# One kernel with two edits: DeltaNet chunks that keep their decays and keys and are merged in pairs, and SSD chunks that start with C·B and its mask

## The chip, the cores and the metric

The kernel runs on one core of a Trainium2 chip. The metric is device time in microseconds of one execution; lower is better. Engines are named as in the profile: PE (TensorE, matrix products), PEld (its weight loads), DVE (VectorE), ACT (ScalarE), POOL (GpSimd) and SP (SyncE, which issues most transfers).

## What is computed

One residual layer over 1024 tokens of width 1024, with 16 meta tokens ahead of them. A normalised input is projected to about 13,400 columns, which feed two token mixers; their gated outputs are merged, projected, added to the input and sent through a gated feed-forward part. Cut to what the change touches:

```python
# gated DeltaNet, per value head and chunk (8 q/k heads, 16 value heads, width 128)
a_low = strict_lower(k_beta @ k.T * decay)           # decay = exp(g_cum[l] - g_cum[s])
t_inv = inverse(a_low + eye)
qk    = (q @ k.T) * decay
v_new = t_inv @ (v*beta) - (t_inv @ (k_beta*exp(g_cum))) @ S
o     = (q*exp(g_cum)) @ S + qk @ v_new
S     = S * exp(g_cum[-1]) + (k*exp(g_cum[-1]-g_cum)).T @ v_new
# SSD, per group of 8 heads and chunk (4 groups, 32 heads of width 64, state 128)
scores = (C @ B.T) * decay
y      = scores @ (x*dt) + (C @ S) * exp(a_cum)
S      = S * exp(a_cum[-1]) + B.T @ (x*dt*decay_to_end)
```

All of it is float32. The large products are made of three products of a rounded high part and its remainder (`hi·hi`, `hi·lo`, `lo·hi`).

## The kernel before

The program is written out in full, with no loop on the chip. A tile framework places buffers from pools and decides, before the program runs, in which order each engine's instructions stand. Each engine then works through its own list in that order. A pool's `bufs` is the number of buffers that a name rotates through, and a new tile waits until the oldest buffer's last reader is done. PSUM has eight banks of 128x512 floats, tagged `psd` (two, for the dense products), `p` (two), and `a`, `b`, `o`, `z` (one each).

There are three stages. In the first, the 1040 columns (16 meta tokens and 8 chunks of 128) are projected, one weight tile of 128 output columns at a time (`dense_u`, `ztile`, `gate_tile`; lines 141 to 143 are the three products), and DeltaNet runs beside it. In the second, SSD runs beside the rest of the projection. In the third come the branch projections and the feed-forward part. "Dense product" below means one matrix product of lines 141 to 143 (in the changed kernel 143 to 145).

A weight tile (512 KB) is loaded by `load_w` into `wraw` (two buffers). ACT rounds it into `whi`, DVE subtracts to get `wlo` (two buffers each), and the tile after the present one is already asked for when a tile starts.

DeltaNet is done for eight sub-heads `i`, each one q/k head with two value heads:

- `dn_conv(i)` makes q, k and v tiles (projection, then a four-tap convolution). `squares` transposes q and k chunk by chunk into the bank `z`, where ACT squares and sums them.
- `dn_p1(i, c)` makes, for each chunk `c`, k·k and the decays of two heads (`decay`: a product with a selecting column and two kinds of ACT instruction), and from them the matrix `W` to be inverted.
- `dn_inv(i)` writes the 32x32 diagonal blocks of `W` to memory, reads them back as `X` with a block in each partition, inverts them on DVE in 30 steps (lines 537 and 539), writes them back (line 541), and reads them into `W` (line 546). Three DVE transposes make `T32` of them (line 550).
- `dn_merge(i, c)` joins the blocks to the whole inverse with products of 96, then 32 and 64 columns (lines 561, 565, 566, 572, 576), each of which waits for an ACT or DVE step after the one before.
- `dn_p2(i, c)` runs the recurrence over the chunks: k·S and q·S (lines 617 and 619), the product with `W` (629), the update of the state (637) and the output (639). It first makes the decays, q·k and the transposed k of the chunk again (lines 608, 609 and 418).
- `dn_z(i, h)` multiplies the finished output by a gate tile; its dense products fill a `psd` bank that is emptied only when the chunks' outputs are ready.

In the program's text a sub-head's conv tiles and `dn_p1` stand after the `dn_p2` of the one before.

Of the kernel before, what the change touches and what calls it, by code (L numbers as in the profile page):

```python
# [92 lines left out]
def body(tc, A):  # L93
# [35 lines left out]

    def load_w(src, kk=KD, room=None):  # L130
# [97 lines left out]
    convp = tkp.tile([128, len(CONV), 5], F32, name="convp")  # L228
    cvp = tc.tile_pool(name="cv", bufs=2)
# [269 lines left out]
    def dn_p1(i, c):  # L499
        d = sub[i]  # L500
        c0, L = cr(c)
        if c == 8:
            d["W"] = sb.tile([128, 8, 2, 128], F32, name="W")
            d["Wm"] = sb.tile([NM, 2, NM], F32, name="Wm")
        kT = d["qk"][:, 1, c0:c0 + L]
        ps = psm("p")
        E = sb.tile([128, 2, 128], F32, name="E")
        pe.matmul(ps[0:L, 256:256 + L], kT, kT, start=True, stop=True)
        decay(E, ps, rowD, selD, 32, (2 * i, 2 * i + 1), c)
        kkm = sb.tile([128, 128], F32, name="kkm")  # L510
        dve.tensor_tensor(kkm[0:L, 0:L], ps[0:L, 256:256 + L], stri[0:L, 0:L], op=ALU.mult)
        N = d["W"][:, c] if c < 8 else d["Wm"]
        for h in range(2):
            dve.scalar_tensor_tensor(N[0:L, h], E[0:L, h, 0:L], d["w"][0:L, c, h:h + 1], kkm[0:L, 0:L],
                                     op0=ALU.mult, op1=ALU.mult)
        nd = nd_dram[i]
        if c in (3, 7):
            for b in range(4):
                r = slice(32 * b, 32 * b + 32)
                for h in range(2):  # L520
                    sp.dma_start(V(nd[0:64], "(c h b) s l -> s c h b l", h=2, b=4)[:, c - 3:c + 1, h, b],
                                 d["W"][r, c - 3:c + 1, h, r])
# [3 lines left out]
    def dn_inv(i):  # L526

        d = sub[i]
        X = sb.tile([66, 32, 32], F32, name="X", bufs=1)
# [18 lines left out]
        for b in range(3):  # L548
            r = slice(32 * b, 32 * b + 32)
            dve.transpose(T32[r, :, r], V(d["W"][r, :, :, r], "s c h l -> s (c h) l"))  # L550

    def dn_merge(i, c):

        d = sub[i]
        W = d["W"]
        ps = psm("p")
        zz = sb.tile([128, 2, 3, 32], F32, name="zz")
        p10 = sb.tile([64, 2, 32], F32, name="p10")
        z4 = V(ps[:, 0:192], "p (h b s) -> p h b s", h=2, b=3)
# [8 lines left out]
        act.copy(W[0:32, c, :, 32:64], p4[0:32])  # L568
        act.copy(W[64:96, c, :, 96:128], p4[64:96])
        p5 = V(ps[:, 256:320], "p (h s) -> p h s", h=2)  # L570
        for h in range(2):
            pe.matmul(p5[64:128, h], W[32:64, c, h, 64:128], p10[32:64, h], start=True, stop=True)
# [665 lines left out]
```

## Time and profile before

| what | us |
|---|---|
| three timed runs | 3000.59, 3000.81, 3009.75 (median 3000.81) |
| profiled execution, its own time | 3007.62 |
| its span, first instruction to last | 3005.8 |
| PE busy in the span | 2916.2 |
| DVE busy | 1974.6 |
| ACT busy | 1324.3 |
| POOL busy | 289.3 |

The span is read along PE. A product's "busy" time in the profile reaches past the start of the next product, because products are pipelined. So what a product costs is read from the distance between starts in the view by time, and not from its mean duration. Instructions with float32 operands on both sides appear as two records per product, transposes and the dense products as one.

### The profile page before, as it was taken

To read this page: it belongs to the slowest core of one execution; us is meant where nothing else is said; L and a number is where in the kernel's file an instruction comes from. 1 tells how busy PE (TensorE), PEld (TensorE's weight loads), DVE (VectorE), ACT (ScalarE), POOL (GpSimd) and SP (SyncE) were. 2 spreads that over 40 slices of the span, in tenths; PEclk is the share of its full clock that TensorE was granted. 3 is DMA by queue.
4 is the path that set the end of the run, shared out by engine and by line. 5 is a ranking of instruction groups with operands and counts; after the bars stand their busy time and mean duration, and the time that the engine had idled before them with its cause. 6 is when DMAs were issued, how large, how long until landed. Compare 5 with 4: busy or idle time off the path is not lost.

```text
span 3005.8 us, 43124 instructions
## 1 busy us (share of the span) xinstructions
PE 2916.2 (97%) x16130; PEld 2452.7 (82%) x16130; DVE 1974.6 (66%) x3858; ACT 1324.3 (44%) x3319; POOL 289.3 (10%) x274
## 2 busy tenths in 40 slices
PE   7899999999999999999999999999999899999997
PEld 6788788888888879878888778888877688888886
DVE  8577787876867855776768653464568655555446
ACT  5546466456554544555546543212235233333213
POOL 2200000000000000001010100000000333330000
PEclk9999999999999999999999999999999899999998
DMA  3111111111211211111011115343353222226312
GB/s 105 43 57 37 50 50 35 58 50 29 64 33 47 68 43 54 35 57 56 33 60 36 70 61 172 102 139 110 112 182 105 97 80 84 81 81 226 96 53 74
DMA packets 119177, 227.32 MB, mean 76 GB/s; under 512 B 46984, under 2 KB 53800, under 8 KB 118968
## 3 DMA queue, kind: packets, MB, share of 16 engines
q1 hardware_dynamic: 117240, 222.47, 22.7%
q8 instruction: 127, 2.08, 0.3%
q10 hardware_dynamic: 1728, 2.10, 0.2%
q14 instruction: 82, 0.67, 0.1%
HBM read 175.14 MB, written 49.38 MB: 75 GB/s over the span
## 4 chain that ended last, share of the span: by engine, by line
PE 84%; DVE 9%; ACT 3%; DMA 1%; issue 1%; POOL 1%; SPq 0%; DVEq 0%; ACTq 0%; POOLq 0%
PE psd L142 15%; PE psd L143 15%; PE psd L141 15%; PE pq_p L1000 1%; PE pq_p L1001 1%; PE pq_p L1002 1%; PE ps_p L561 1%; PE ps_o L746 1%; PE pq_psd L1001 1%; PE ps_o L639 1%; PE pq_psd L1002 1%; PE pq_psd L1000 1%; PE ps_a L629 1%; PE ps_a L617 1%; PE ps_o L619 1%
## 5 line engine op out<-in xcount | busy, mean ns | idle before, releaser
L142 PE MATMUL psd<-u_lo,whi 128*128 128x512 f32 (+3 forms) x2136 | 770.8, 361 | 3.4 <-DVE u_lo L150 2.3
L141 PE MATMUL psd<-u_hi,whi 128*128 128x512 f32 (+3 forms) x2136 | 764.9, 358 | 1.6 <-ACT raw L374 1.6
L143 PE MATMUL psd<-u_hi,wlo 128*128 128x512 f32 (+3 forms) x2136 | 758.0, 355 | 4.0 <-DVE wlo L135 4.0
L134 ACT CAST whi<-wraw 128x1024 fp32r<-128x1024 f32 (+2 forms) x197 | 188.0, 955 | 649.1 <-PE psd L142 459.6
L142 PEld LDWEIGHTS psd<-u_lo,whi 128*128 128x128 f32 x2136 | 409.6, 192 | 41.3 <-issue 6.8
L143 PEld LDWEIGHTS psd<-u_hi,wlo 128*128 128x128 f32 x2136 | 406.1, 190 | 36.7 <-DVE wlo L135 4.5
L141 PEld LDWEIGHTS psd<-u_hi,whi 128*128 128x128 f32 x2136 | 405.2, 190 | 37.6 <-issue 4.0
L135 DVE TENSOR_TENSOR wlo<-wraw,whi 128x1024 fp32r<-128x1024 f32 (+2 forms) x197 | 217.8, 1106 | 153.5 <-ACT whi L134 147.4
L143 PE MATMUL psd<-blk,wlo 128*128 128x512 f32 x512 | 199.7, 390 | 1.2 <-DVE wlo L135 1.2
L141 PE MATMUL psd<-blk,whi 128*128 128x512 f32 x512 | 199.4, 390 | 0.0
L142 PE MATMUL psd<-blk,whi 128*128 128x512 f32 x512 | 199.4, 389 | 0.0
L374 ACT COPY raw<-psd 128x256 f32<-128x256 f32 x165 | 73.3, 444 | 93.1 <-PE psd L143 89.5
L143 PEld LDWEIGHTS psd<-blk,wlo 128*128 128x128 f32 x512 | 96.2, 188 | 21.8 <-DVE wlo L135 2.0
L906 DVE TENSOR_TENSOR part<-part,psd 128x512 f32<-128x512 f32 x96 | 65.7, 684 | 72.0 <-PE psd L143 72.0
L142 PEld LDWEIGHTS psd<-blk,whi 128*128 128x128 f32 x512 | 96.2, 188 | 20.1
L141 PEld LDWEIGHTS psd<-blk,whi 128*128 128x128 f32 x512 | 96.2, 188 | 19.8
L984 POOL TENSOR_TENSOR sw<-wraw 128x512 f32<-128x512 f32 x44 | 68.4, 1554 | 352.0 <-DMA wraw<-w_gu 240.5
L700 DVE TENSOR_TENSOR xdt<-ps_z,dtb 128x512 f32<-128x512 f32 (+1 forms) x36 | 24.8, 690 | 105.3 <-PE ps_z L697 105.3
L539 DVE TENSOR_TENSOR X<-X,itmp 66x30 f32<-66x30 f32 (+14 forms) x240 | 85.2, 355 | 5.2
L537 DVE TENSOR_TENSOR itmp<-X 66x30 f32<-66x30 f32 (+14 forms) x240 | 81.6, 340 | 5.8 <-DMA X<-nd 0.4
L99 POOL TENSOR_TENSOR qk<-raw,qk 128x400 f32<-128x400 f32 x16 | 30.4, 1900 | 537.6 <-ACT raw L380 423.3
L421 ACT ACTIVATE Es<-ps_p,cum 128x128 f32<-128x128 f32 x256 | 75.3, 372 | 11.1 <-PE ps_p L418 11.0
(686 smaller groups left out, 6277.7 us busy)
## 6 DMA issues: line engine op xcount, KB each, us to landing
wraw<-w_in SPq DMA_DIRECT2D x105, 512.0 KB, 3.3
wraw<-w_gu SPq DMA_DIRECT2D x48, 512.0 KB, 3.3
wraw<-w_br SPq DMA_DIRECT2D x36, 512.0 KB, 3.4
c<-hc SPq DMA_DIRECT2D x22, 512.0 KB, 2.7
hc<-c SPq DMA_DIRECT2D x22, 512.0 KB, 5.9
wraw<-w_dn SPq DMA_DIRECT2D x40, 256.0 KB, 2.6
g<-zt SPq DMA_DIRECT2D x32, 256.0 KB, 2.1
y_d<-zt SPq DMA_DIRECT2D x32, 256.0 KB, 2.0
```

Source lines behind the costliest of these rows:

```text
L134: act.copy(hi[:, 0:kk], raw[:, 0:kk])
L135: dve.tensor_tensor(lo[:, 0:kk], raw[:, 0:kk], hi[:, 0:kk], op=ALU.subtract)
L141: pe.matmul(ps[:, 0:n], hi[:, wk0 + k], ahi(k), start=(k == 0), stop=False)
L142: pe.matmul(ps[:, 0:n], hi[:, wk0 + k], alo(k), start=False, stop=False)
L143: pe.matmul(ps[:, 0:n], lo[:, wk0 + k], ahi(k), start=False, stop=(k == kk - 1))
L374: dense_u((name, lambda ps, p0, p1: act.copy(raw[:, 3 + p0:3 + p1], ps)))
L421: act.activation(E[0:L, i, 0:L], ps[0:L, 128 * i:128 * i + L], AF.Relu, bias=cum[0:L, c, h0 + h:h0 + h + 1], scale=-1.0)
L537: dve.tensor_tensor(t, X[:, 0:j, j:j + 1].broadcast_to([66, j, m]), X[:, j:j + 1, j + 1:32].broadcast_to([66, j, m]), op=ALU.mult)
L539: dve.tensor_tensor(X[:, 0:j, j + 1:32], X[:, 0:j, j + 1:32], t, op=ALU.add)
L906: dve.tensor_tensor(part[:, m, cs], part[:, m, cs], ps, op=ALU.add)
L984: pool.tensor_tensor(t, x, y, op=op)
L1000: pe.matmul(ps, w[0][:, k], y[0][:, k], start=start and k == 0, stop=False, skip_group_check=not start)
```

## The change

DeltaNet: `dn_p1` now also makes q·k, masks it and multiplies it into the decays `E`, which are kept for `dn_p2` (eight buffers). `squares` copies the transposed k out of the bank `z` four chunks at a time, and `dn_p2` and `dn_meta` read this copy. `dn_merge` joins two chunks (four matrices) at once. `W` is held in two halves with three buffers, `X` and `T32` share one buffer, `dn_p1` alternates between the banks `p` and `b`, and the blocks come back from memory in 16 transfers in place of 8. SSD: a chunk starts with C·B, its mask and the decays; the transposed input and the product for the state come later. The raw weight tile `wraw` has one buffer through the first two stages and two after them.

```diff
-        raw = wp.tile([128, KD, 128], F32, name="wraw", bufs=2)
+        raw = raws[0].tile([128, KD, 128], F32, name="wraw")
...
+    wrp = tc.tile_pool(name="wr1", bufs=1)
+    raws[0] = wrp.__enter__()
...
 squares:
+                pv = lambda c: ps[0:cr(c)[1], 128 * (c % 4):128 * (c % 4) + 128]
                 for c in cc:
                     c0, L = cr(c)
-                    pv = ps[0:L, 128 * (c % 4):128 * (c % 4) + 128]
-                    pe.transpose(pv, qk[:, j, c0:c0 + L], ident)
-                    act.activation(pv, pv, AF.Square, accum_out=ss[0:L, j, c:c + 1])
+                    pe.transpose(pv(c), qk[:, j, c0:c0 + L], ident)
+                if j == 1 and len(cc) > 1:
+                    d["kt", cc[0] // 4] = kt = sb.tile([128, 4, 128], F32, name="kt", bufs=3)
+                    act.copy(kt, V(ps, "p (c k) -> p c k", c=4))
+                elif j == 1:
+                    act.copy(d["ktm"], pv(8))
+                for c in cc:
+                    act.activation(pv(c), pv(c), AF.Square, accum_out=ss[0:cr(c)[1], j, c:c + 1])
...
 dn_p1:
-        ps = psm("p")
-        E = sb.tile([128, 2, 128], F32, name="E")
+        ps = psm("pb"[c % 2])
         pe.matmul(ps[0:L, 256:256 + L], kT, kT, start=True, stop=True)
+        if c < 8:
+            pe.matmul(ps[:, 384:512], kT, qT, start=True, stop=True)
+            E = d["E", c] = sb.tile([128, 2, 128], F32, name="E", bufs=8)
...
+            qkm = sb.tile([128, 128], F32, name="qkm")
+            dve.tensor_tensor(qkm, ps[:, 384:512], tri, op=ALU.mult)
...
+            dve.tensor_tensor(E, E, qkm.unsqueeze(1).broadcast_to([128, 2, 128]), op=ALU.mult)
...
 dn_inv:
-                sp.dma_start(d["W"][r, :, h, r], bv(xd_dram[i])[:, :, h, b])
+                for k in range(2):
+                    sp.dma_start(d["W"][k][r, :, h, r], bv(xd_dram[i])[:, 4 * k:4 * k + 4, h, b])
...
 dn_merge:
-        for h in range(2):
-            pe.matmul(p4[0:32, h], zz[32:64, h, 0], W[32:64, c, h, 32:64], start=True, stop=True)
-            pe.matmul(p4[64:96, h], zz[96:128, h, 2], W[96:128, c, h, 96:128], start=True, stop=True)
-            dve.transpose(p10[32:64, h], p4[0:32, h])
...
+        for h, (k, e) in enumerate(ch):
+            pe.matmul(p4[0:32, h], zz[32:64, h, 0], W[32:64, k, e, 32:64], start=True, stop=True)
+            pe.matmul(p4[64:96, h], zz[96:128, h, 2], W[96:128, k, e, 96:128], start=True, stop=True)
+        dve.transpose(V(p10[32:64], "p h s -> p (h s)"), ps[0:32, 384:512])
...
 dn_p2:
-        ps = psm("b")
-        E = sb.tile([128, 2, 128], F32, name="E2")
-        pe.matmul(ps[:, 256:384], kT, qT, start=True, stop=True)
-        pe.transpose(ps[:, 384:512], kT, ident)
-        decay(E, ps, rowD, selD, 32, (2 * i, 2 * i + 1), c)
-        qkm = sb.tile([128, 128], F32, name="qkm")
-        kt = sb.tile([128, 128], F32, name="kt")
-        dve.tensor_tensor(qkm, ps[:, 256:384], tri, op=ALU.mult)
-        act.copy(kt, ps[:, 384:512])
-        dve.tensor_tensor(E, E, qkm.unsqueeze(1).broadcast_to([128, 2, 128]), op=ALU.mult)
+        E, kt = d.pop(("E", c)), d["kt", c // 4][:, c % 4]
...
 ssd_chunk:
+        if c < 8:
+            pe.matmul(ps[:, 128:256], Bc, Cc, start=True, stop=True)
+            cbm = sb2.tile([128, 128], F32, name="cbm")
+            dve.tensor_tensor(cbm, ps[:, 128:256], tri, op=ALU.mult)
...
+        x, xdt, xh, xl = inputs()
         S = d["S"]
...
+        pst = states(xh, xl)
         dve.tensor_tensor(t1, t1, j4(py), op=ALU.add)
...
             dn_merge(i, c)
-            dn_merge(i, c + 1)
             dn_p2(i, c)
             dn_p2(i, c + 1)
```

How this moves instructions on PE is shown at three places. In these rows `L` numbers are lines of the kernel concerned; `psd<-u_hi,whi` and its two companions are dense products, `ps_z<-ident,qk` is a transpose of `squares`.

First, PE in `squares` of one sub-head, the last chunks. Before:

```order
L446 MATMUL ps_z<-ident,qk 128x128
L142 MATMUL psd<-u_lo,whi 128x384
L143 MATMUL psd<-u_hi,wlo 128x384
L141 MATMUL psd<-u_hi,whi 128x384
L446 MATMUL ps_z<-ident,qk 16x128
```

The same work of a sub-head in the changed kernel:

```order
L143 MATMUL psd<-u_hi,whi 128x256
L452 MATMUL ps_z<-ident,qk 128x128 x4
L144 MATMUL psd<-u_lo,whi 128x256
L145 MATMUL psd<-u_hi,wlo 128x256
L143 MATMUL psd<-u_hi,whi 128x256
```

Single transposes between three dense products each have become runs of four.

Second, PE at the first merges of sub-head 3, from the product for the meta tokens' state (`ps_a<-vd`) on. Before, with the products of one chunk (two heads) in each step:

```order
L594 MATMUL ps_a<-vd,kt 128x256
L565 MATMUL ps_p<-W,zz 32x32
L566 MATMUL ps_p<-W,zz 32x32
L565 MATMUL ps_p<-W,zz 32x32
L566 MATMUL ps_p<-W,zz 32x32
L143 MATMUL psd<-u_hi,wlo 128x512
L141 MATMUL psd<-u_hi,whi 128x512
L142 MATMUL psd<-u_lo,whi 128x512
L617 MATMUL ps_a<-S,qk 128x256
L572 MATMUL ps_p<-p_5607,W 64x32 x2
L572 MATMUL ps_p<-p_5627,W 64x32 x2
L619 MATMUL ps_o<-S,qk 128x256
```

In the changed kernel, where a step holds two chunks:

```order
L623 MATMUL ps_a<-vd,ktm 128x256
L604 MATMUL ps_p<-p_5348,W 64x32 x4
L591 MATMUL ps_p<-T_5162,W 128x96 x3
L637 MATMUL ps_a<-S,qk 128x256
L608 MATMUL ps_p<-W,zz 64x64 x4
L639 MATMUL ps_o<-S,qk 128x256
L591 MATMUL ps_p<-T_5162,W 128x96
L649 MATMUL ps_a<-v,W 128x128 x2
```

Pieces of four stand where pieces of two stood, and q·k, the transposed k and the decays no longer stand between them.

Third, PE in the recurrence of sub-head 6, between the products with the state (`ps_a<-S,qk`) of chunks 5 and 6 (before: chunks 6 and 7). Before:

```order
L617 MATMUL ps_a<-S,qk 128x256
L619 MATMUL ps_o<-S,qk 128x256
L576 MATMUL ps_p<-W,zz 64x64 x2
L446 MATMUL ps_z<-ident,qk 128x128
L142 MATMUL psd<-u_lo,whi 128x384
L143 MATMUL psd<-u_hi,wlo 128x384
L629 MATMUL ps_a<-v,W 128x128 x2
L141 MATMUL psd<-u_hi,whi 128x384
L142 MATMUL psd<-u_lo,whi 128x384
```

In the changed kernel:

```order
L637 MATMUL ps_a<-S,qk 128x256
L639 MATMUL ps_o<-S,qk 128x256
L649 MATMUL ps_a<-v,W 128x128 x2
L659 MATMUL ps_o<-v_9485,E 128x128
L657 MATMUL ps_a<-vd,kt 128x256
L659 MATMUL ps_o<-v_9485,E 128x128
L496 MATMUL ps_z<-ident,cacc 128x128 x4
```

At this place no dense product stands between the steps of the recurrence any more.

## Rows read from the trace of the kernel before

**Rows 1.** The page: busy time of engines, and the granted clock in 40 slices.

```profile
PE 2916.2 (97%) x16130; PEld 2452.7 (82%) x16130; DVE 1974.6 (66%) x3858; ACT 1324.3 (44%) x3319; POOL 289.3 (10%) x274
...
PEclk9999999999999999999999999999999899999998
```

**Rows 2.** Windows: stretch, its length, busy time of each engine (instructions), granted clock.

```profile
130.00:1130.00 1000.00, 993.23 (x6361) 841.29 (x6360) 746.58 (x2083) 545.34 (x1815) 44.17 (x73) 0.99 0.16 48
703.50:713.50 10.00, 10.00 (x50) 7.85 (x50) 3.40 (x15) 4.08 (x16) 0.11 (x1) 0.50 0.01 2
829.80:843.20 13.40, 13.40 (x63) 10.75 (x63) 4.74 (x17) 5.51 (x23) 0.00 (x0) 0.50 0.00 1
...
1790.00:3005.00 1215.00, 1169.51 (x5194) 964.88 (x5193) 682.16 (x950) 366.71 (x591) 158.56 (x108) 0.98 0.34 112
```

**Rows 3.** PE by time near 1017 us: start, length, line, records.

```profile
1016.91 0.38 PE L508 MATMUL ps_p<-qk 128*128 128x128 f32 x2
1017.13 0.28 PE L418 MATMUL ps_p<-rowD,selD 96*128 96x128 bf16 x2
1017.24 0.50 PE L670 MATMUL ps_z<-ident,v 128*128 128x128 f32 x3
1017.59 0.49 PE L508 MATMUL ps_p<-qk 128*128 128x128 f32 x2
```

**Rows 4.** PE by time near 431 us, a lone transpose among dense products.

```profile
430.72 0.33 PE L446 MATMUL ps_z<-ident,qk 128*128 128x128 f32 x1
430.81 0.42 PE L142 MATMUL psd<-u_lo,whi 128*128 128x384 f32 x1
431.07 0.34 PE L143 MATMUL psd<-u_hi,wlo 128*128 128x384 f32 x1
431.24 0.33 PE L141 MATMUL psd<-u_hi,whi 128*128 128x384 f32 x1
431.51 0.33 PE L446 MATMUL ps_z<-ident,qk 128*128 128x128 f32 x1
```

**Rows 5.** Groups by line: the decays of `dn_p2` on PE (count, busy, mean ns).

```profile
L418 PE MATMUL ps_b<-rowD,selD 96*128 96x128 bf16 x128 | 19.6, 224 | 0.0
```

**Rows 6.** PE by time: first merge of sub-head 6, k·S of its chunk 4.

```profile
944.34 0.32 PE L561 MATMUL ps_p<-T,W 128*128 128x96 f32 x1
...
974.45 0.43 PE L617 MATMUL ps_a<-S,qk 128*128 128x256 f32 x1
```

**Rows 7.** Groups by line: DVE in `dn_p2` and `dn_p1` (count, busy, mean ns).

```profile
L514 DVE SCALAR_TENSOR_TENSOR W<-E,w,kkm 128x128 f32<-128x128 f32 x128 | 40.4, 345 | 1.8 <-ACT E L424 1.0
L623 DVE SCALAR_TENSOR_TENSOR v<-ps_a,ecum,v 128x128 f32<-128x128 f32 x128 | 39.7, 347 | 21.9 <-PE ps_a L617 21.2
L642 DVE SCALAR_TENSOR_TENSOR S<-S,clast,ps_a 128x128 f32<-128x128 f32 x128 | 39.3, 344 | 43.7 <-PE ps_a L637 43.5
L633 DVE TENSOR_TENSOR vd<-ps_a,wd 128x256 f32<-128x256 f32 x64 | 27.1, 424 | 29.5 <-PE ps_a L629 28.5
L661 DVE TENSOR_TENSOR v<-v,f 128x1024 f32<-128x1024 f32 x16 | 19.6, 1223 | 0.4
L511 DVE TENSOR_TENSOR kkm<-ps_p,stri 128x128 f32<-128x128 f32 (+1 forms) x72 | 19.3, 270 | 7.9 <-ACT E L421 7.5
L160 DVE TENSOR_TENSOR rs_to<-rs_to,x 128x8 f32<-128x8 f32 x32 | 6.1, 191 | 0.6
```

**Rows 8.** All engines by time: from the last `W` of sub-head 7 to its first merge.

```profile
1021.67 0.61 DVE L514 SCALAR_TENSOR_TENSOR W<-E,w,kkm 128x128 f32<-128x128 f32 x2
...
1032.96 0.20 DVE L537 TENSOR_TENSOR itmp<-X 66x30 f32<-66x30 f32 x1
...
1057.79 0.18 DVE L539 TENSOR_TENSOR X<-X,itmp 66x30 f32<-66x30 f32 x1
...
1061.90 3.78 SPq L546 DMA_DIRECT2D W<-xd  x8
...
1068.97 0.41 PEld L561 LDWEIGHTS ps_p<-T,W 128*128 128x128 f32 x3 [0.36 <-DVE T L550]
```

More of the change, by code (lines that the diff above doesn't have):

```diff
@@ L428, in body, with xt @@
     sb = dn.__enter__()
-    T32 = sb.tile([128, 16, 96], F32, name="T32", bufs=1)
-    pool.memset(T32, 0.0)
+    def xt(name):
+        return sb.tile([128, 1536], F32, name=name, tag="XT", bufs=1)
     sub = [dict() for _ in range(NSUB)]
@@ L435, in dn_conv @@
         qk = d["qk"] = sba.tile([128, 2, TT], F32, name="qk")
+        d["ktm"] = sb.tile([NM, 128], F32, name="ktm")
         ss = sb.tile([128, 2, 9], F32, name="ss")
@@ L528, in dn_inv @@
         d = sub[i]
-        X = sb.tile([66, 32, 32], F32, name="X", bufs=1)
+        X = V(xt("X")[0:66, 0:1024], "p (a b) -> p a b", b=32)
         pool.memset(X[64:66], 0.0)
@@ L545, in dn_inv @@
             for h in range(2):
-                sp.dma_start(d["W"][r, :, h, r], bv(xd_dram[i])[:, :, h, b])
+                for k in range(2):
+                    sp.dma_start(d["W"][k][r, :, h, r], bv(xd_dram[i])[:, 4 * k:4 * k + 4, h, b])
         sp.dma_start(d["Wm"], V(xd_dram[i][64:66, 0:NM, 0:NM], "h s l -> s h l"))
-        for b in range(3):
-            r = slice(32 * b, 32 * b + 32)
-            dve.transpose(T32[r, :, r], V(d["W"][r, :, :, r], "s c h l -> s (c h) l"))
+        T32 = d["T32"] = V(xt("T32"), "p (a b) -> p a b", b=96)
@@ L552, in dn_merge @@
+        pool.memset(T32, 0.0)
+        for k in range(2):
+            for b in range(3):
+                r = slice(32 * b, 32 * b + 32)
+                dve.transpose(T32[r, 8 * k:8 * k + 8, r], V(d["W"][k][r, :, :, r], "s c h l -> s (c h) l"))
     def dn_merge(i, c):
         d = sub[i]
-        W = d["W"]
+        W, T32 = d["W"][c // 4], d["T32"]
+        T32 = T32[:, 8 * (c // 4):8 * (c // 4) + 8]
+        c = c % 4
+        ch = [(c + h // 2, h % 2) for h in range(4)]
         ps = psm("p")
-        zz = sb.tile([128, 2, 3, 32], F32, name="zz")
@@ L568, in dn_merge @@
[L568 to L572, printed above, removed]
+        zz = sb.tile([128, 4, 3, 32], F32, name="zz")
+        p10 = sb.tile([64, 4, 32], F32, name="p10")
+        for h, (k, e) in enumerate(ch):
+            pe.matmul(ps[:, 96 * h:96 * h + 96], W[:, k, e], T32[:, 2 * k + e], start=True, stop=True)
@@ L573, in dn_merge @@
+        act.copy(W[0:32, c:c + 2, :, 32:64], c4(p4[0:32]))
+        act.copy(W[64:96, c:c + 2, :, 96:128], c4(p4[64:96]))
+        ps = psm("p")
+        p5 = V(ps[:, 0:128], "p (h s) -> p h s", h=4)
+        for h, (k, e) in enumerate(ch):
+            pe.matmul(p5[64:128, h], W[32:64, k, e, 64:128], p10[32:64, h], start=True, stop=True)
         dve.tensor_tensor(zz[64:128, :, 0], zz[64:128, :, 0], p5[64:128], op=ALU.add)
-        p6 = V(ps[:, 320:448], "p (h s) -> p h s", h=2)
-        for h in range(2):
-            pe.matmul(p6[0:64, h], V(zz[64:128, h, 0:2], "p b s -> p (b s)"), W[64:128, c, h, 64:128],
+        p6 = V(ps[:, 128:384], "p (h s) -> p h s", h=4)
@@ L577, in dn_merge @@
+        for h, (k, e) in enumerate(ch):
+            pe.matmul(p6[0:64, h], V(zz[64:128, h, 0:2], "p b s -> p (b s)"), W[64:128, k, e, 64:128],
                       start=True, stop=True)
-        act.copy(W[0:64, c, :, 64:128], p6[0:64])
+        act.copy(W[0:64, c:c + 2, :, 64:128], c4(p6[0:64]))
     def dn_meta(i):
         d = sub[i]
-        kT = d["qk"][:, 1, 0:NM]
         ps = psm("a")
-        pe.transpose(ps[0:NM, 0:128], kT, ident)
         for h in range(2):
@@ L693, in ssd_chunk @@
         h8 = lambda t: V(t, "p (h k) -> p h k", h=8)
-        x = d["x"][:, :, c0:c0 + L]
-        px = psm("z")
-        for j in range(4):
-            pe.transpose(px[0:L, 128 * j:128 * j + 128], x[:, j], ident)
-        xdt = sb2.tile([128, 512], F32, name="xdt")
-        xde = sb2.tile([128, 512], F32, name="xde", bufs=1)
-        dve.tensor_tensor(h8(xdt[0:L]), h8(px[0:L]), bc(dtb), op=ALU.mult)
-        dve.tensor_tensor(h8(xde[0:L]), h8(xdt[0:L]), bc(dte), op=ALU.mult)
         Bc, Cc = d["B"][:, c0:c0 + L], d["C"][:, c0:c0 + L]
@@ L747, in ssd_chunk @@
                       start=True, stop=True)
+        pst = states(xh, xl)
         dve.tensor_tensor(t1, t1, j4(py), op=ALU.add)
+        S2 = d["S"] = sb2.tile([128, 512], F32, name="Ss")
+        dve.tensor_tensor(h8(S2), h8(S), bc(clast), op=ALU.mult)
+        dve.tensor_tensor(S2, S2, pst, op=ALU.add)
         for j in range(4):
@@ L844, in body @@
     cvp.__exit__(None, None, None)
+    wrp.__exit__(None, None, None)
     tkpp.__exit__(None, None, None)
+    raws[0] = st.enter_context(tc.tile_pool(name="wr2", bufs=2))
     banks[:] = ["psd", "a", "psd", "b", "o"]
@@ L993, in raw_w @@
     def raw_w(src, i):
-        r = wp.tile([128, KD, 128], F32, name="wraw", bufs=2)
+        r = raws[0].tile([128, KD, 128], F32, name="wraw")
         sp.dma_start(r, src)
```

70 lines of the change are left out of this document (41 added, 29 removed).

## The prediction

> **What bounds the kernel now.** I read the page first. PE is busy 2916.2 of 3005.8 us, DVE 1974.6, ACT 1324.3, and the granted clock is at nine tenths or more in all slices but two [rows 1]. Then the windows by stage: in the DeltaNet stretch from 130 to 1130 us PE is busy 993 of 1000 us, with DVE at 747 and ACT at 545 [rows 2]. So PE never runs dry there: dense products stand between the steps of DeltaNet wherever one would wait. Whatever the change saves on DVE and ACT is worth nothing by itself; what it takes from PE counts, as long as PE finds other work. From 1790 us on the orders of PE, ACT and DVE are the same in both kernels, so I leave that stretch of 1215 us [rows 2] alone.
>
> **What a product costs PE.** I go by starts in the view by time. In [rows 3] k·k (two records) takes 1017.13 - 1016.91 = 0.22 us, two decays 0.11 (0.055 each), three transposes in a run 0.35 (0.117 each). In [rows 4] a lone transpose stands among dense products of 384 columns: the pattern of one transpose and three dense products repeats after 0.79 us. A dense product in the middle of it takes 431.24 - 431.07 = 0.17 to 0.175, so the lone transpose costs 0.79 - 0.525 = 0.263 us, which is 0.146 more than in a run. The dense product after it shows the larger part: 0.26 in place of 0.175. A lone transpose is two changes of kind (dense to transpose and back), so a change costs about 0.07 us.
>
> [...]
>
> **Removed from PE.** The decays of `dn_p2`: 128 products [rows 5] at 0.055 = 7.0 us. The transposes of k: 64 in `dn_p2` and 8 in `dn_meta` at 0.117 = 8.4 us. q·k only moves. Together 15.4 us.
>
> **Kept together on PE.** I sorted PE's order by kind (dense, full float32 product, transpose, decay, 32- and 64-row pieces, the SSD products of 64 columns) and counted how often a product follows one of another kind: 1930 times before, 1371 after. Runs of transposes in `squares` go from 144 to 51, the rest comes from the merges and from `dn_p2`. 559 changes at 0.07 = 39 us. The bounds: 0 if only lone transposes were dear (then 93 x 0.146 = 14 us remain), and 48 at the 0.086 that the dense product after a transpose shows. So PE's work shrinks by 15.4 + 39 = 54 us (29 to 63).
>
> **Where that gain goes.** The number of dense products between the first merges of two sub-heads in PE's order tells what PE does with the time. Before: 378, 365, 381, 364, 384, 350, 360. After: 387, 408, 394, 409, 407, 409, and then 182. Up to the first merge of sub-head 6 PE has done 197 more dense products than before, at about 0.2 us (0.175 for 384 columns, 0.235 for 512) 39 us. The saving up to there is six sub-heads' decays and transposes, 11.6 us, and 404 changes, 28 us: 40 us. They cancel, and this merge comes where it came, at 944.3 us [rows 6]. The dense work is brought forward, and in the period of sub-head 6 it is used up.
>
> There the chain of steps decides. In the kernel before, k·S of chunk 4 comes 30.1 us after the first merge [rows 6], and the first merge of sub-head 7 another 94.5 us later, at 1068.97 [rows 8]; PE filled that with 331 dense products and 132 others. The new order has 161 and 79: 161 x 0.235 + 79 x 0.18 = 52 us. But the chain can't shrink to that. From [rows 7], DVE has to do for each of four chunks 2 x 0.347 + 2 x 0.344 + 2 x 0.42 = 2.2 us (8.9), for each of eight new `dn_p1` chunks 2 x 0.345 + 0.424 + 2 x 0.27 = 1.65 us (13.2), two normalisations of finished chunks with 1.22 and some 14 small instructions of 0.17 each (7.2), and about 7.5 us (an estimate from instructions of like sizes) of key factors, value tiles and gate tiles: 37 us to the last `W`. Then, as before, 10.7 us to the first inversion step (stores and load of the blocks), 25.0 us of inversion to 1057.97, and 11.0 us to the merge, with 0.36 us of which PE waits for the transposes [rows 8]. The blocks now take 16 transfers at 3.78 / 8 = 0.47 us; those of the first three row blocks must land before the last transposes, four of them additional, plus half the rest: 2.5 us. Sum 37 + 10.7 + 25 + 11 + 2.5 = 86 us, where PE has 52 us of work: a hole of 34 us. Bounds: 82 if DVE is never late, 94.5 if the chain is as long as before.
>
> So the first merge of sub-head 7 comes at 944.3 + 30 + 86 = 1060 us, 9 us earlier (13 to 0). Afterwards PE is full again, and gets there with 19 dense products more done (4.5 us), 16 decays and 8 transposes of sub-head 7 less (1.8 us), and 62 changes of kind less up to the end (4.3 us): 10.6 us.
>
> **Priced at nothing.** The shared buffer of `X` and `T32` needs a clearing by POOL in each sub-head, which runs while the blocks travel; POOL is busy 44 of 1000 us [rows 2]. The single `wraw`: PE works on one tile while the next lies split in `whi` and `wlo`, so a load has a whole tile's time to land; SP's order keeps it so. Without that cover each late tile would show as a gap before a dense product. The reordered SSD chunk has the same instructions; its 64-column products follow their decays later than before, so I expect no new wait, and count no gain.
>
> **Sum.** 9 + 10.6 = 19 us faster (10 to 24; up to 36 if the two stretches at half clock that the clock's rival names below vanish). Against the profiled execution's own time, 3007.6, that is 2988.6. That execution lies 6.8 us above the median of the timed runs, so for the median I take 3000.8 - 19 = 2982 us.
>
> **Rivals.**
> - *The whole gain arrives.* No hole: 3000.8 - 54 = 2947 us. For it: PE is the bound in every other period of the stage. Against it: the 182 dense products where 360 stood, and the chain above, whose last 49 us after the last `W` contain no step that the change shortens.
> - *The clock takes the rest.* PE ran at half clock, 0.50, in two stretches of 10.0 and 13.4 us at the first merges of sub-heads 4 and 5, though it had work all the time [rows 2]. That cost about half of them, 12 us. A hole of 34 us makes a third likely: if PE's 14 us of work between chunk 4 and the last `W`, which lies in the chain, runs at half clock, the chain grows by 14 us: 2982 + 14 = 2996, no change that can be told. Against it: the two old stretches may vanish as well. [...]
> - *Slower: every period is bound by its chain.* `E` has eight buffers and `W` three halves, so the last `dn_p1` of a sub-head waits for the last chunk of the one before, and the inversion comes after it. If the six earlier periods, for which the new order has some 117 us of work each, all took the 124.6 us of the last period (944.3 to 1068.97), that is 6 x 7.6 = 46 us: 2982 + 46 = 3028. From 4.7 us a period on ((19 + 9) / 6) it decides for slower. Against it: the orders hold 387 to 409 dense products there, and before the change PE did not wait at a first merge for more than the 0.36 us of [rows 8].
>
> **How the numbers follow.** The forecast gets 0.55 (own range 2965 to 2991), the whole gain 0.11, the clock's or no change 0.23, slower 0.11. About 0.3%, 9 us, is what a measurement can tell from no change. Faster: 0.55 + 0.11 = 0.66; same 0.23; slower 0.11. The range leaves out the slower case and the far half of the whole gain: 2953 to 3003.
>
> **What would show it.** Right: PE's product count falls by the 128 decays and 72 transposes; a window over the period of sub-head 6 shows PE at about two thirds, with waits for DVE at `ps_z` and at the first merge, and the first merge of sub-head 7 near 1060 us; the stretch from the branch projections on lasts as long as before. Wrong: PE at 99% there (the whole gain), PE idle in each of the first six periods before its first merge (slower), half clock over tens of us, or gaps before dense products that DMA of `wraw` ended.

## The result, and the profile after

The changed kernel took 2979.86 us (median of four runs, 2975.82 to 2982.60) where the kernel before took 3000.70 in runs beside it (median of four, 3000.22 to 3009.75). The ratio on record is 0.9907, 95% interval 0.9891 to 0.9922; the two medians alone give 0.9931, since three of these four runs of the kernel before came out at 3000, where its median beside the experiments is 3006.9 to 3008.3. The gain is thus 21 us by the medians and 28 by the ratio. The forecast was 2982, 19 us less. The profiled execution took 2982.60 us, its span is 2980.7, 25.1 less than before. The time is near the forecast, but two steps on the way to it are not.

The page of the changed kernel, busy time and granted clock, answers to [rows 1]:

```profile
PE 2862.5 (96%) x15930; PEld 2426.1 (81%) x15930; DVE 1941.0 (65%) x3754; ACT 1249.6 (42%) x2951; POOL 297.1 (10%) x281
...
PEclk9999999999999999999999999999999999999998
```

PE is busy 53.7 us less, close to the 54 that the prediction took from it. Some 5 us of them are clock (an estimate): stretches at a granted clock of 0.50 add up to 94.0 us in the trace before and to 84.3 in this one, and half of the difference is counted. The span shrank by 25.1 only, so PE now stands idle 28.6 us longer than before. The windows of the changed kernel, columns as in [rows 2] (behind the clock, the busy share of the DMA engines and GB/s), show where:

```profile
130.00:1130.00 1000.00, 957.80 (x6240) 831.69 (x6240) 733.61 (x1985) 469.95 (x1448) 54.03 (x80) 0.99 0.16 49
223.60:958.70 735.10, 710.09 (x4708) 622.01 (x4707) 557.84 (x1496) 356.31 (x1093) 44.39 (x64) 1.00 0.16 48
958.70:1064.10 105.40, 90.62 (x541) 71.79 (x542) 70.34 (x230) 39.08 (x132) 2.37 (x3) 0.92 0.17 53
1015.70:1029.30 13.60, 7.49 (x26) 5.50 (x27) 7.77 (x19) 1.19 (x2) 0.00 (x0) 0.50 0.34 106
1765.00:2980.70 1215.70, 1172.52 (x5201) 966.97 (x5199) 681.77 (x952) 367.62 (x592) 160.11 (x108) 0.98 0.33 112
```

Between the first merges of sub-heads 0 and 6 (the second line) PE is idle 735.10 - 710.09 = 25.0 us, and in the period of sub-head 6 (the third) 14.8. Before, the same two stretches together had 4.9, all of them ahead of the first merge of sub-head 6 (at 944.3 there). Windows of the kernel before, to that merge and to the next:

```profile
228.00:944.30 716.30, 711.37 (x4646) 607.86 (x4644) 553.28 (x1541) 397.82 (x1328) 32.14 (x52) 0.98 0.16 47
228.00:1069.00 841.00, 836.07 (x5406) 710.75 (x5404) 642.38 (x1797) 460.88 (x1537) 35.70 (x58) 0.99 0.16 49
```

The last line of the changed kernel's windows answers to the last of [rows 2]: nothing changed there.

The waits of PE in the changed kernel between 224 and 960 us (total, times, longest) name no single culprit:

```profile
PE psd L143 <- ACT raw L378: 9.1, 19, 1.0
PE ps_p L591 <- DMA W<-xd: 3.9, 4, 1.4
PE ps_p L591 <- DVE T L578: 2.7, 2, 2.2
PE ps_z L690 <- DVE zt L400: 2.0, 3, 1.2
```

The view by time of the changed kernel, with the lines that answer to [rows 6, 8] and, ahead of them, some of sub-head 1's recurrence (its first merge is at 344.2 us):

```profile
372.01 0.61 PE L657 MATMUL ps_a<-vd,kt 128*128 128x256 f32 x2
...
372.66 0.59 ACT L455 COPY kt<-ps_z 128x512 f32<-128x512 f32 x1 [0.25 <-PE ps_a L657]
...
384.79 0.17 DVE L475 TENSOR_TENSOR w<-dtb,ss 128x18 f32<-128x18 f32 x1
...
958.65 0.32 PE L591 MATMUL ps_p<-T,W 128*128 128x96 f32 x1 [1.44 <-DMA W<-xd]
...
989.58 0.38 PE L637 MATMUL ps_a<-S,qk 128*128 128x256 f32 x1
...
1017.65 0.61 DVE L536 SCALAR_TENSOR_TENSOR W<-E,w,kkm 128x128 f32<-128x128 f32 x2
...
1027.36 0.20 DVE L561 TENSOR_TENSOR itmp<-X 66x30 f32<-66x30 f32 x1
...
1052.99 0.18 DVE L563 TENSOR_TENSOR X<-X,itmp 66x30 f32<-66x30 f32 x1
...
1064.13 0.24 PE L591 MATMUL ps_p<-T,W 128*128 128x96 f32 x1
```

The first merge of sub-head 6 comes at 958.65, 14.3 us later than in [rows 6]; that of sub-head 7 at 1064.13, 4.8 us earlier than in [rows 8]; from there to the end it is 20.2 us less. The first three lines turned out to matter for the length of the periods (decays_again_kt4 below): the copy of the second four kept keys of sub-head 2 starts when the state product of sub-head 1's chunk 3 ends, and the factor `w`, without which no `W` can be made, comes 12 us after that. All seven later sub-heads show it: the copy stands 27.6 to 30.9 us after the first merge of the sub-head before, within 0.3 us of the end of that product.

### The profile page after: what moved, and what is told of

The parts are those of the page before. It is cut to its first block, busy times and chain, and to the rows that moved or that the text cites. A ratio compares the mean times of both kernels' runs of the same rounds, so it can differ in the third digit from the quotient of the medians.

```text
span 2980.7 us, 42122 instructions
## 1 busy us (share of the span) xinstructions
PE 2862.5 (96%) x15930; PEld 2426.1 (81%) x15930; DVE 1941.0 (65%) x3754; ACT 1249.6 (42%) x2951; POOL 297.1 (10%) x281
## 5 line engine op out<-in xcount | busy, mean ns | idle before, releaser
L144 PE MATMUL psd<-u_lo,whi 128*128 128x512 f32 (+3 forms) x2136 | 758.8, 355 | 3.7 <-DVE u_lo L152 2.3
L137 DVE TENSOR_TENSOR wlo<-wraw,whi 128x1024 fp32r<-128x1024 f32 (+2 forms) x197 | 218.8, 1111 | 124.6 <-ACT whi L136 124.6
L561 DVE TENSOR_TENSOR itmp<-X 66x30 f32<-66x30 f32 (+14 forms) x240 | 89.9, 374 | 5.8
L723 DVE TENSOR_TENSOR cbm<-ps_p,tri 128x128 f32<-128x128 f32 x32 | 9.3, 292 | 104.3 <-PE ps_p L721 104.1
L397 ACT ACTIVATE zt<-psd 128x512 f32<-128x512 f32 x64 | 38.1, 596 | 87.3 <-PE psd L145 66.5
```

The lines of the kernel that those rows point to most:

```text
L144: pe.matmul(ps[:, 0:n], hi[:, wk0 + k], alo(k), start=False, stop=False)
L561: dve.tensor_tensor(t, X[:, 0:j, j:j + 1].broadcast_to([66, j, m]), X[:, j:j + 1, j + 1:32].broadcast_to([66, j, m]), op=ALU.mult)
```

## The experiments

All ratios are to the kernel before, run beside each (whose median there is 3006.9 to 3008.3 us, so ratios are compared and not times), with the 95% interval.

### What each part is worth

The changed kernel's `ssd_chunk` in the kernel before:

```diff
+            pe.matmul(ps[:, 128:256], Bc, Cc, start=True, stop=True)
...
+        x, xdt, xh, xl = inputs()
...
+        pst = states(xh, xl)
```

> The kernel before with the SSD chunk in the new order and nothing else. Theory (the new order saves by itself): in the traces a chunk with its 72 dense products takes 16.4 us after the change where it took 17.0, and the 15 waits of some 0.67 us before the first product with the decays (9.4 us together) give way to 16 of 0.30 us before the product for the state (4.8 us). From the first product with decays to the last the changed kernel took 5.0 us less, with five dense products more (1 us). So 3000.7 - 6 = 2995 us (2993 to 2997). Rival, as the prediction priced it: nothing, 2999 to 3003, and the shorter chunks come from DeltaNet's part.

Measured: 0.9973 (0.9963 to 0.9982), 8 us. In the trace the stretch from sub-head 7's first merge to the last product with the decays is 8.0 us shorter as well (709.3 in place of 717.3). Waits of PE, the first view of the kernel before from 1233 to 1786 us, the second of this one from 1230 to 1778:

```profile
PE ps_o L746 <- DVE Es L732: 7.4, 11, 0.7
PE ps_o L746 <- ACT raw L374: 1.9, 3, 0.7
```

```profile
PE ps_a L724 <- ACT xh L146: 4.5, 14, 0.3
```

With the products of the inputs between the decays' steps and the products that read them, a wait of 0.7 us per chunk becomes one of 0.3. That is 4.8 of the 8 us; the rest is not placed. The prediction's nothing was wrong.

One buffer for `wraw` alone:

```diff
-        raw = wp.tile([128, KD, 128], F32, name="wraw", bufs=2)
+        raw = raws[0].tile([128, KD, 128], F32, name="wraw")
```

> The kernel before with one buffer for wraw in the first two stages and nothing else. By the prediction's price of nothing: 2999 to 3003 us, and no wait before a dense product that a load of wraw ended. Rival: each of the some 100 tiles waits for its load for a few tenths of a us, 3010 to 3030.

Measured: 0.9979 (0.9970 to 0.9989), 6 us faster rather than nothing. No wait of PE for a load of `wraw` shows, which is what the price rested on. In the profile the first merge comes 3.6 us earlier (224.4) because 14 dense products fewer stand ahead of it; the rest I can't place.

Runs of four transposes alone:

```diff
                 for c in cc:
                     pe.transpose(pv(c), qk[:, j, c0:c0 + L], ident)
+                for c in cc:
                     act.activation(pv(c), pv(c), AF.Square, accum_out=ss[0:cr(c)[1], j, c:c + 1])
```

> The kernel before, where the four transposes of a bank in squares stand together and the four squares of ACT after them, and nothing else. PE's order has 94 runs of transposes fewer and 167 changes of kind fewer. Theory (a change of kind costs 0.07 us, and PE is the bound): 167 x 0.07 = 11.7 us, by lone transposes 94 x 0.146 = 13.7: 2987 to 2990 us. Rival (the chain of DeltaNet's steps sets the periods): the time stays, 2999 to 3003, and the freed time shows as waits of PE before first merges or before transposes.

Measured: 0.9987 (0.9976 to 0.9998), 4 us. PE's busy time fell from 2916.2 to 2905.5, 10.7 us or 0.064 for each of the 167 changes, but between the first merges of sub-heads 0 and 7 it is idle 839.80 - 830.45 = 9.4 us in place of 4.9. Both theories hold in part: about half of that saving turns into waits. The price is near only with the clock counted in: stretches at 0.50 add up to 8.1 us less here (85.9 in place of 94.0), and without half of these some 6.6 us or 0.04 a change remain (an estimate).

Joining one chunk at a time in the changed kernel, that is, all of the change but the pairs:

```diff
 dn_merge:
-        ch = [(c + h // 2, h % 2) for h in range(4)]
...
             dn_merge(i, c)
+            dn_merge(i, c + 1)
```

> The changed kernel with one chunk joined at a time in dn_merge, as before the change; all else as after it. PE's order has 203 changes of kind more than the changed kernel's 1478. Theory A (each costs 0.07 us of PE's time, and PE is the bound): 14 us, 2994 us (2990 to 2998). Theory B (periods are as long as their chain, and PE has 4 us of waits in each to absorb it): part of the 14 us shows as fewer waits, 2982 to 2989.

Measured: 1.0060 (1.0044 to 1.0076), median 3026.03. Without the pairs the change is a loss. Undoing them costs 1.5%, three times theory A's 14 us. Windows of this kernel behind the first merges of sub-heads 2 (477.9), 3 (617.3) and 6 (992.3):

```profile
479.10:499.60 20.50, 20.50 (x97) 15.27 (x96) 4.16 (x16) 5.18 (x21) 0.00 (x0) 0.50 0.07 26
622.40:632.70 10.30, 10.30 (x44) 7.79 (x41) 1.98 (x7) 2.72 (x10) 0.00 (x0) 0.50 0.01 2
997.90:1008.10 10.20, 10.20 (x44) 7.50 (x44) 1.94 (x8) 2.61 (x10) 0.00 (x0) 0.50 0.00 1
```

PE works through the narrow products of the merges, busy all the time, and its granted clock is 0.50 of full for 10 to 20 us. Over the whole trace such stretches add up to 133.7 us, in the changed kernel to 84.3. The other runs agree: the mean granted clock is 0.977 to 0.980 in all five of no_pairs and 0.986 to 0.987 in the four of the changed kernel. If half of such a stretch is lost (an estimate), that is 25 us of the 46.

Pairs in the kernel before (with one `wraw`, for room):

```diff
+        ch = [(c + h // 2, h % 2) for h in range(4)]
...
             dn_merge(i, c)
-            dn_merge(i, c + 1)
```

> The kernel before with merged pairs and one wraw buffer (two don't leave room), and nothing else. one_raw alone was at 0.9979. PE's order has 163 changes of kind fewer than one_raw. Theory A (pairs are worth their changes, 0.07 us each, and PE is the bound): 11 us less than one_raw, a ratio of 0.994 to before. Theory B (pairs are worth in themselves what undoing them in the changed kernel cost, 1.5%, by a shorter run of narrow products that then holds the clock up): 0.983, with less than 10 us at half clock behind first merges. Theory C (no_pairs was slow for a reason that lies in the kept decays: its periods are as long as their chain): 0.994 as A, with PE idle under 10 us between the first merges of sub-heads 0 and 7.

Measured: 0.9884 (0.9869 to 0.9899), median 2972.64: if anything faster than the changed kernel (the two intervals just overlap), with three of its parts left out. The pairs alone give 0.95% over one_raw, 28 us, between theories A and B; C's idle time holds. Windows of one_raw, then of this kernel (from the first merge of sub-head 0 to that of 7, then half clock behind first merges):

```profile
224.40:1067.70 843.30, 839.50 (x5420) 714.43 (x5418) 642.25 (x1798) 461.24 (x1538) 35.63 (x58) 0.98 0.16 49
698.70:715.70 17.00, 17.00 (x81) 13.05 (x81) 6.54 (x26) 6.91 (x28) 0.11 (x1) 0.50 0.00 1
828.40:842.00 13.60, 13.60 (x65) 10.96 (x64) 4.93 (x18) 5.59 (x23) 0.00 (x0) 0.50 0.00 1
```

```profile
222.20:1039.50 817.30, 812.38 (x5421) 702.17 (x5419) 621.47 (x1686) 447.05 (x1426) 36.35 (x58) 0.99 0.16 50
227.20:234.00 6.80, 6.80 (x37) 5.57 (x37) 1.66 (x5) 3.11 (x10) 0.00 (x0) 0.50 0.00 0
350.10:356.90 6.80, 6.80 (x33) 5.93 (x32) 2.21 (x6) 3.21 (x10) 0.00 (x0) 0.50 0.01 1
```

PE is busy 27 us less and idle 4.9 us in all: here nearly the whole of PE's saving arrives. Some 8 of the 27 are clock (an estimate, half of the difference): between these merges stretches at 0.50 add up to 30.7 us in one_raw and to 13.7 here.

All parts but the kept decays, q·k and keys and the buffers that go with them (the kernel before with the edits of ssd_only, one_raw, squares_four and pairs_raw1):

> The kernel before with pairs, one wraw buffer, the runs of four transposes and the new SSD chunk: all parts of the change but the kept decays, q.k and keys. PE's order has the 200 products of before and 1684 changes of kind (2046 before, 1478 after). Theory A (the parts add up, and the kept decays and keys are worth their 15.4 us of PE's time): one_raw 6 us, SSD 8, squares 4, pairs 11, together 29 us of 3008, a ratio of 0.990, and with the kept parts the changed kernel would then have to be at 0.985, where it is at 0.991. Theory B (keeping decays and keys pulls dense products forward, and their waits, 40 us of PE idle between the first merges of sub-heads 0 and 7 where there were 5, eat what it saves): 0.985 to 0.991, with PE idle under 12 us there, as fast as the changed kernel or faster. Rival (keeping is worth its whole price): over 0.995.

Measured: 0.9866 (0.9845 to 0.9887), median 2963.19. Between the first merges of sub-heads 0 and 7 PE is idle 834.00 - 826.20 = 7.8 us. The profiled execution took 2982.84 us, 20 above the median, and has a long stretch at half clock behind the first merge of sub-head 6 (921.9), with PE busy all the time:

```profile
927.30:958.00 30.70, 30.70 (x170) 25.67 (x169) 8.44 (x26) 11.89 (x43) 0.00 (x0) 0.50 0.00 1
```

So what `dn_p2` no longer does in the changed kernel, 15.4 us of PE's work, did not make it faster: with all that came along (`W` in halves and the 16 transfers, the buffer shared by `X` and `T32`, two banks for `dn_p1`) the changed kernel is some 0.4% slower. That is theory B. This run does not tell these parts from each other.

### What takes the gain away

A gate tile moved into the hole:

```diff
-GATES_DN = (1, 1, 1, 0, 1, 0, 1, 0, 3)
+GATES_DN = (1, 1, 1, 0, 1, 0, 1, 1, 2)
```

> The changed kernel with one gate tile (48 dense products of 512 columns) moved from behind sub-head 7 to between its inversion and its merges: PE's order then has 237 dense products between the first merges of sub-heads 6 and 7 in place of 182. Theory (the hole in that period is PE without work, 14.8 us of 104): 55 x 0.235 = 12.9 us of work fill it, the first merge of sub-head 7 stays within 3 us of 1064, and what comes after it is 13 us shorter: 2980 - 10 = 2970 us (2966 to 2974). Rival (the dense products stand ahead of steps of the chain on PE, and DVE's additional tile work delays the inversion): the first merge comes as much later as work was moved, 2978 to 2983.

Measured: 0.9896 (0.9880 to 0.9912), median 2976.62. The windows of this kernel, the period of sub-head 6 and the stretch from there to the first SSD product with decays:

```profile
957.90:1064.40 106.50, 98.63 (x597) 80.38 (x598) 73.55 (x234) 40.04 (x135) 2.36 (x3) 0.95 0.19 60
1064.40:1207.90 143.50, 140.07 (x944) 130.20 (x942) 80.59 (x142) 67.19 (x155) 8.02 (x14) 0.98 0.13 45
```

The work fits in (7.9 us idle in place of 14.8) and the merge stays where it was, at 1064.4. The stretch behind it is 143.5 us where the changed kernel has 149.3, 5.8 us of the 13: PE now waits 3.4 us there, and runs at 0.50 from 1133.6 to 1140.5. About 3 us remain, too little to tell from the changed kernel by these intervals.

The store of the gate tile on another queue:

```diff
-        ztile(f"zd{j}", yT, dnw, lambda hf, t: sp.dma_start(y_dram["d", j][:, 512 * hf:512 * hf + 512], t))
+        ztile(f"zd{j}", yT, dnw, lambda hf, t: pool.dma_start(y_dram["d", j][:, 512 * hf:512 * hf + 512], t))
```

> The changed kernel with the store of the finished gate tile (y_d) issued by POOL and not by SP. In the changed kernel PE waited 20 times, 9.2 us together, before the first dense product of a tile between 224 and 1064 us: one of the two psd banks is held by a gate tile whose buffers wait for a store that stands in SP's queue behind the 16 stores of blocks (nd), so that the tiles of q and k use one bank alone and wait for its emptying, 0.5 us each. Theory (PE is still the bound there): most of the 9.2 us goes, 2971 to 2975 us. Rival (the periods are as long as the chain of recurrence, stores, inversion and merge): the waits turn up before the first merges, and the time stays at 2978 to 2982.

Measured: 0.9910 (0.9895 to 0.9924). The waits from 223 to 1064 us stayed:

```profile
PE psd L143 <- ACT raw L378: 9.2, 18, 1.8
```

So the stores' place in SP's queue is not what holds the bank, and my theory falls. That store now waited on POOL for DVE's product of the gate, which waits for finished chunks.

The first half's blocks loaded first:

```diff
-        for b in range(4):
+        for k, b in [(k, b) for k in range(2) for b in range(4)]:
             r = slice(32 * b, 32 * b + 32)
             for h in range(2):
-                for k in range(2):
...
```

> The changed kernel, where the 8 transfers that bring back the inverted blocks of chunks 0 to 3 stand ahead of the 8 of chunks 4 to 7 (before, they alternate). The first merge needs only the first eight. Theory (from the second period on a period is as long as its chain of recurrence, stores, inversion and merge, and PE's 25 us of waits in the six periods from 224 to 960 us, with 14.8 us in the last, come from that): the first merge comes 8 x 0.47 = 3.7 us earlier in each of the periods, and PE has about 4 us of waits in each to give: 2980 - 7 x 3 = 2959 us (2954 to 2967). Rival (PE is the bound, and the waits are accidents of order): only the 6.6 us of waits right before first merges can go, 2973 to 2980.

Measured: 0.9921 (0.9905 to 0.9936), median 2983.66, no gain. From the inversion's end to the merge it now takes 7.5 to 9.5 us in place of 10.5 to 12.5. But the order of PE that comes with it has 3426 dense products ahead of sub-head 7's first merge and not 3467; that merge comes 8 us earlier (1056.0) with 41 products, some 9.6 us, still to do, PE is idle as long (38.1 us), and stretches at 0.50 add up to 107 us. Neither theory's number came; a shorter last link of the chain was no help.

The low part of the projection's weight tiles on POOL (`ptt` is a `tensor_tensor` of POOL):

```diff
-        dve.tensor_tensor(lo[:, 0:kk], raw[:, 0:kk], hi[:, 0:kk], op=ALU.subtract)
+        if late:
+            ptt(lo, raw, hi, ALU.subtract)
+        else:
+            dve.tensor_tensor(lo[:, 0:kk], raw[:, 0:kk], hi[:, 0:kk], op=ALU.subtract)
...
-                ahead[n] = load_w(A["w_in"][TIDX[n]])
+                ahead[n] = load_w(A["w_in"][TIDX[n]], late=True)
```

> The changed kernel, where POOL and not DVE makes the low part (wlo) of each weight tile of the projection. In the trace of the changed kernel DVE has no idle time in the inversion of sub-head 2 (412.8 to 454.5 us, 41.7 us): 21.9 us are the inversion's own steps, 12 to 13 us the taps of q, k and v tiles, 4.9 us four low parts. Theory (the dense tiles brought forward put their DVE work into the inversion and so lengthen the chain that bounds the period): the inversion gets some 5 us shorter in each period, the recurrence some 2 us, and PE's waits of 4 us in a period and 14.8 us in the last go for the larger part: 2980 - 25 = 2955 us (2948 to 2967). Rival (PE is the bound, or POOL, at about 5 us for a tile by 1.94 us for 400 columns, delivers the low parts late): 2977 to 2990, with waits before products with wlo.

Measured: 1.0156 (1.0138 to 1.0173), median 3054.74, far outside both. Four views of this kernel follow: the window of the DeltaNet stretch, with 61.5 us of idle PE and a mean clock of 0.96; the two largest waits of PE from 223 to 1064.5 us; a multiplication of DVE with both operands in SBUF (ns: least, median, most); and the largest wait of PE from 1267 to 1839 us:

```profile
230.10:1098.00 867.90, 806.44 (x5232) 699.55 (x5230) 637.84 (x1682) 394.56 (x1224) 146.59 (x109) 0.96 0.15 46
```

```profile
PE psd L146 <- DVE zt L401: 11.4, 5, 4.6
PE ps_p L594 <- DVE T L581: 9.2, 4, 5.8
```

```profile
L739 DVE TENSOR_TENSOR xde<-xdt,dte x34: 672/2062/2121, 1279.8 to 1836.2; 128x512 f32<-128x512 f32 x31, 16x512 f32<-16x512 f32 x3
```

```profile
PE ps_o L778 <- DVE Es L766: 23.5, 27, 1.3
```

The median of that multiplication was 684 ns in the changed kernel. Of all 36 of the trace, the 28 that meet a POOL instruction take 1891 ns in the mean, the other 8 684. In the DeltaNet stretch DVE has 43 instructions fewer than in the changed kernel between the same merges (1682 and 1725) and is busy longer all the same (637.84 and 628.18 us). So POOL gave DVE no relief: where the two met, this multiplication took 2.8 times as long, and PE's largest waits are for DVE. POOL itself needed 2.4 us for a tile (mean of the stretch), half of what was expected.

Decays made again, keys kept in three buffers; then the same with four:

```diff
 dn_p1:
-        ps = psm("pb"[c % 2])
+        ps = psm("p")
...
-            E = d["E", c] = sb.tile([128, 2, 128], F32, name="E", bufs=8)
+            E = sb.tile([128, 2, 128], F32, name="E")
...
 dn_p2:
+        ps = psm("b")
+        E = sb.tile([128, 2, 128], F32, name="E2")
+        pe.matmul(ps[:, 256:384], kT, qT, start=True, stop=True)
+        decay(E, ps, rowD, selD, 32, (2 * i, 2 * i + 1), c)
...
```

The second has this edit besides:

```diff
-                    d["kt", cc[0] // 4] = kt = sb.tile([128, 4, 128], F32, name="kt", bufs=3)
+                    d["kt", cc[0] // 4] = kt = sb.tile([128, 4, 128], F32, name="kt", bufs=4)
```

> The changed kernel, where the recurrence makes decays and q.k again as before the change; the keys are kept, in three buffers of four chunks. PE's order has 128 products more than the changed kernel and 1595 changes of kind (1478). Theory A (the copy of the second four kept keys waits for the third buffer until chunk 3 of the sub-head before has updated its state; in the changed kernel it starts 27.6 to 30.8 us after each first merge, within 0.3 us of the end of that product, and the factors of the keys and all of dn_p1 come after it): the wait is still there, a period still takes 118 to 125 us, PE is idle 25 us or more between the first merges of sub-heads 0 and 7, and the time is 2980 to 2990. Theory B (the eight buffers of the kept decays hold up dn_p1): the wait is gone, periods of 102 to 116 us as in pairs_raw1, 2955 to 2968.

> decays_again with four buffers for the kept keys in place of three (there is room since the decays are not kept), and nothing else. Theory A (the third buffer of keys is what delays dn_p1): the last k.k of a sub-head stands up to 16 products ahead of the last k.S of the sub-head before, where it stood 45 to 62 behind it; X is read 6 us earlier, PE is idle under 12 us between the first merges of sub-heads 0 and 7, and with the 72 transposes of k less than all_but_kept (8.4 us, and 65 changes of kind less) the time is 2950 to 2960. Theory B (the eight buffers of decays): no difference to decays_again, within 5 us.

Measured: 0.9870 (0.9854 to 0.9885), median 2968.02, and 0.9822 (0.9809 to 0.9836), median 2953.09. The first has the periods of its theory A (119 to 122 us, once 133), the time of the upper end of B (2968), and an idle time of PE, 19.7 us, under A's 25. The second came where theory A put it, with 13.1 us of idle PE. Windows between the first merges of sub-heads 0 and 7, with three buffers and with four:

```profile
221.60:1063.60 842.00, 822.29 (x5426) 718.04 (x5427) 631.65 (x1729) 448.86 (x1397) 47.17 (x67) 0.98 0.16 49
```

```profile
222.30:1030.40 808.10, 794.99 (x5350) 698.57 (x5351) 623.09 (x1707) 446.41 (x1381) 45.77 (x66) 0.99 0.16 50
```

And with four buffers the copy and the factor of sub-head 2, by time (the first merge of sub-head 1 is at 343.2 here):

```profile
311.55 0.59 ACT L455 COPY kt<-ps_z 128x512 f32<-128x512 f32 x1 [0.75 <-PE ps_z L452]
```

```profile
327.53 0.17 DVE L475 TENSOR_TENSOR w<-dtb,ss 128x18 f32<-128x18 f32 x1
```

The factor stands 16 us ahead of the first merge, where it stood 40.6 behind it in the changed kernel. After the first merges of sub-heads 0 to 3, `X` is read 55.3 to 56.6 us later in place of 63.2 to 64.0, and the periods of sub-heads 1 to 3 take 109 to 116 us in place of 121 to 123 (the three after them 118, 109 and 124). One buffer is worth 15 us in this kernel; in the changed kernel itself no run tried a fourth.

Making the decays again is worth 11 us besides, by the ratios, though PE is busy 9.4 us longer (2871.9); it is idle 20 us less. This does not come as shorter periods: from the first merge of sub-head 0 to that of 7 it takes 842.0 us, in the changed kernel 840.5. But PE has done 3517 dense products by the latter merge, and 3467 in the changed kernel; 50 x 0.235 = 12 us (an estimate). Why there was room for them I didn't separate; the multiplications by q·k that had moved into `dn_p1`, the eight buffers of `E` and the banks of `dn_p1` are candidates.

decays_again_kt4 beats both kernels, the changed one by 0.9%. It also beats all_but_kept, which makes the transposes of k again, by 0.44%: with a buffer more, keeping the keys pays, together with what came along with it.

## Why the prediction came out

- **PE's work, -54.** Right: 53.7, of which some 5 are clock. Its parts are not: transposes in runs are worth less (10.7 us for 167 changes, not 11.7 to 13.7, and some of it clock), the merges more. From one_raw to pairs_raw1 PE's busy time over the whole trace fell from 2917.2 to 2882.7, 34.5 us; stretches at 0.50 shrank by 22.5 us, which is some 11 of them (an estimate, by half). The other 23 for 163 changes of kind would be 0.14 each, twice the 0.07 of the sum. (0.79 - 0.525 in the working of that price is 0.265, not 0.263, which changes nothing.) The 0.07 was read at lone transposes [rows 4]; that the 32- and 64-row pieces of the merges cost the same was the author's estimate, and these two runs do not bear it out: 0.04 to 0.064 us a change in squares_four, some 0.14 for the pairs. Why the latter cost more no run shows.
- **Where that gain goes.** This step failed. The count of dense products brought forward is right, but "they cancel, and this merge comes where it came, at 944.3" took PE for the bound of every period. PE's work does cancel: it is busy 710.1 us between the first merges of sub-heads 0 and 6, and was 711.4. But the sum had no term for waits: each of the six periods took 121 to 124 us with 3 to 5 us of idle PE, 25.0 in all where it was 4.9, and the merge came at 958.7. The chain set the periods, since the kept keys' third buffer put the factors behind chunk 3 of the recurrence. decays_again_kt4 shows that for the kernel that makes its decays again; for the changed kernel it is taken over from there, and what the eight buffers of `E` add is open.
- **The hole, 34 us and a chain of 86.** The place is right and the size is off: PE is idle 14.8 us (busy 86% of the period, not two thirds), and the chain from k·S of chunk 4 to the merge took 74.6, less than the lower bound of 82, for which the prediction shows no working. DVE needed 28.7 us and not 37 to the last `W`; stores and load 9.1, inversion 25.8, and 11.0 to the merge, as in [rows 8]: the additional transfers' 2.5 us are not there. With the merge before it late by 14, the first merge of sub-head 7 came at 1064.1 and not at 1060.
- **Behind it, -10.6.** It was -20.2. SSD's new order gives 8 of the difference (ssd_only), and seven q·k products of sub-head 7, which now stand earlier, were forgotten (1.5 us at the 0.22 of a k·k in [rows 3]).
- **Priced at nothing.** True for POOL's clearing and for `wraw`'s loads, for which no wait of PE shows; wrong for SSD, and one_raw gained 6 us that the sum does not have.
- **The clock.** As that rival said, the hole got a stretch at 0.50 (1015.7 to 1029.3), and the two old ones shrank to one of 3.4 us. In the DeltaNet stretch from 224 to 1110 us they add up to 27 us before and after: no net effect here. That rival's step from a hole to half clock has no row behind it, and the traces show both: at 0.50 PE was busy 6.38 of 20.47 us in the kernel before (68.50 to 88.97) and 7.49 of 13.60 in the hole, but all of the 10.0 and 13.4 us of [rows 2], 20.50 of 20.50 in the merges of no_pairs and 30.70 of 30.70 in all_but_kept. What lowers the clock was not shown.
- **Slower.** Its mechanism is what happened in six periods, at 121 to 124 us where it said 124.6; it named `E`'s buffers, where the runs show a buffer of keys and leave `E`'s open. The six periods together are 19 us longer than before (735.1 and 716.3), 3.1 each, and the rival needed 4.7 each to decide; the short period of sub-head 6 (105.4 us) and SSD outweighed them.

So the forecast of 2982 was met by luck, by errors that nearly cancel: up to the first merge of sub-head 6, 14 us lost; 10 gained in the period of sub-head 6 and 10 behind it. That is 6 us more than the forecast of 19, and the spans do differ by 25.1.

## What to carry to other kernels

A value that is kept for later needs buffers for the whole time between its making and its last use, in both of the overlapping iterations; with one too few, its producer waits for the iteration before, and with it all that is computed beside it. Ask which copy stands first on the chain, and when its oldest buffer comes free. And where PE is full, keep its narrow products in few, long runs: that was worth 28 us here, while 15 us of products left out, with the buffers that they got, were worth less than nothing.

## What was not expected of the hardware

- DVE's product with both operands in SBUF (128x512, wlo_pool) took 684 ns alone and 1891 in the mean when POOL worked at the same time.
- The granted clock fell to 0.50 for 10 to 20 us behind first merges in no_pairs although PE was busy throughout. With merged pairs such stretches were shorter in the changed kernel (3.4 us) and in pairs_raw1 (6.8 us), but not always: one lasted 17.1 us in decays_again (from 710.7 us) and one 30.7 in all_but_kept, with PE busy throughout.
